# Decoder trunk on one core: second layer's tokens reordered in blocks of 128, softmax statistics exchanged by VectorE transposes, eleven query pairs projected ahead instead of eight

## The chip, the core and the metric

The kernel is one program on one core of a Trainium2 chip. Five engines run their own instruction queues in order and meet at semaphores: PE (TensorE, matrix products into PSUM), DVE (VectorE), ACT (ScalarE), POOL (GpSimd) and SP (SyncE, which here only issues DMA transfers). The metric is device time in microseconds of one execution; a smaller time is better. Before the change it is 1128.27 us, the median of three runs (1128.21, 1128.27, 1128.74).

## The reference

A sequence of 1024 tokens with 1024 features goes through two layers. The first is gated linear attention with 4 heads. The second is attention with 8 query heads over one shared set of keys and values (2 key/value heads), and it alone matters for most of the change:

```python
SWA_GROUPS = ((128, 1), (512, 4), (2048, 16))       # (window, dilation)
...
for gi, (window, dilation) in enumerate(SWA_GROUPS):
    o_g, lse_g = dilated_window_attention(q[:, :, gi], k_sh[:, :, gi], v_sh[:, :, gi], window, dilation)
    outs.append(o_g)
    lses.append(lse_g)
wts = jax.nn.softmax(jnp.stack(lses, axis=0), axis=0)
o = jnp.sum(wts[..., None] * jnp.stack(outs, axis=0), axis=0)
...
return (o.astype(x.dtype) * jax.nn.silu(g)) @ w_out
```

Each query head attends three times: with every token, with every 4th and with every 16th (groups 0, 1 and 2). Each gives an output, a row maximum and a row sum. A softmax over the three log-sums weighs the three outputs of a token. So the statistics of one token, which the three groups compute in three orders of the tokens, have to meet in one place, and the weights have to go back to each group's order.

## The kernel before, in words

Activations lie features by tokens, 128 features on the partitions. A projection is a product of three matmuls per block of 128 features (`mm3`): a float32 operand is split into a high and a low float32r half, and high x high, high x low and low x high are summed. `project` makes one head's projection, 2 halves of 512 tokens x 8 blocks x 3 = 48 matmuls of 128x512. `seven` makes the projections of two heads together with 7 products in place of 8 (sums of quarters of the weights and of the activations): 7 x 4 x 3 = 84 matmuls in place of 96. The list `EARLY` (line 42) names the query heads and groups that go through `seven` ahead of the attention; their results are written to DRAM (`qd`) and loaded again as `Q`. Before, it holds 8 pairs, groups 2 and 1 of all eight heads, so group 0 is left to `project`, one head at a time, inside the attention loop. With 3 pairs of keys there are 11 jobs.

The program's stages by the trace: first layer to about 436 us, the values and sums for `seven` to 503, the `seven` jobs to 712.4, attention to about 1029, and the output projection with the last normalization to the end.

Attention runs head by head (u = 0 to 7). `scores(u)` computes for each group and block the products of queries and keys (PSUM tiles `lv`, two of them), then on DVE adds the mask (`bmask`, `rmask`) and finds the row's extreme in one instruction, then on ACT takes the exponential and its row sum. Extremes and sums go to `sts` (groups 0 and 1) and `nat` (group 2). Then before the change SP moves them: `sts` to DRAM (`std`), from there to `nat` in the order of group 2; DVE and ACT make the weights `ew`; SP writes them to DRAM (`cwd`) and loads them as `cw` in the orders of groups 0 and 1. `attend(u)` multiplies each block `P` by its weight (16 instructions on whichever of DVE, ACT and POOL), transposes blocks on PE (`ms`), copies with triangle masks (`PT`), multiplies with the values into `po`, and adds into `og`. `g_proj(u)` projects the gate (48 matmuls, PSUM tile `acc`) and multiplies it in. `scores(u+1)` is recorded ahead of `attend(u)`.

The order on each engine is not written by hand. Every operation is recorded, and `Sched.order` (a planner with a table of costs, `cost`, and of latencies) places them one by one: at each step the operation that can start first, by program order where several can. Operations recorded under `vp`, `va` or `vap` may go to one of two or three engines, whichever the planner finds ends first. All instructions are issued from one line (465), so the trace is read by the names of the tiles.

Tiles of `small(..., "a", n)` are a pool of n buffers of 128x512: the `P` of groups 1 and 2, sums, and two diagonal blocks.

Of the kernel before, what the change touches and what calls it, by code (L numbers as in the profile page):

```python
# [53 lines left out]
def _rearr(x, pattern, **sizes):  # L54
# [567 lines left out]
def trunk(tc, xT, wP, wA, wA12, wAv3, w2, wO, wK, wV0, wV12, wB, wOB, par_d,  # L622
# [126 lines left out]
    def og_page(kt, pool):  # L749
# [5 lines left out]
        return ogs[kt]  # L755

    def layer_a(t2, t1, after):
# [46 lines left out]
        def evac_g(h, c, half, acc):  # L804
            S.vector.tensor_copy(H[h]["sg"][:, c, hs(half)], acc)
# [210 lines left out]
        def chunks(h, g):  # L1016
# [6 lines left out]
            for c in range(4):  # L1023
                cc = 4 * g + c
                cs = slice(c * 128, c * 128 + 128)
                for e in range(2):
                    es = slice(e * 128, e * 128 + 128)
                    S.tensor.matmul(po[e][:, cs], v[g][:, c, es], AT[:, cc, :], start=True, stop=(cc == 0))
                    if cc:
                        S.tensor.matmul(po[e][:, cs], St[:, es], blk(qe, cc), start=False, stop=True)  # L1030
# [70 lines left out]
    def out_ln(layer, r, w_of, res, emit):  # L1101
# [14 lines left out]
        for et in range(NK):  # L1116
# [4 lines left out]
            t = small("rt", "a", 13)[:, :n]  # L1121
# [29 lines left out]
    def out_ln_rows(j, wo, gam, bet):  # L1151
        xr = [small("res", tag, 2) for tag in ("t1", "t2")]
        rt = [small("rt", "a", 13) for _ in range(2)]
# [19 lines left out]
        mv = hp.tile([128, 2], F32, name="lnmv", bufs=2)  # L1173
        S.vector.bn_aggr(out=mv, in_=st)
        R = hp.tile([128, 1], F32, name="lnR", bufs=2)
# [16 lines left out]
    vd = dram.tile([T, 256], F32, name="vd")  # L1192
    vd3 = [dram.tile([T, 128], F32, name=f"vd3{c}") for c in range(2)]
    ogB = [dram.tile([128, T], F32, name=f"ogB{k}") for k in range(NK)]
    std = [dram.tile([2, 2, T], F32, name=f"std{k}") for k in range(NK)]
    cwd = [dram.tile([2, T], F32, name=f"cwd{k}") for k in range(NK)]
    DIL = (1, 4, 8)
# [3 lines left out]
    def to_group(pg, g, half):  # L1201
        if g == 2:
            return pg.rearrange("p (e a n) -> p n a e", e=16, a=8)[:, half * 4:half * 4 + 4]
        n = 512 // DIL[g]
        return pg.rearrange("p (r i) -> p i r", r=DIL[g])[:, half * n:half * n + n, :]

    def tok_view(ap, g):
        if g == 2:
            return ap.rearrange("p (n a e) -> p n a e", n=4, a=8)
        return ap.rearrange("p (i r) -> p i r", r=DIL[g])  # L1210

    def layer_b(xs, early):
        bmask = hp.tile([128, 256], F32, name="bmask", bufs=1)
# [4 lines left out]
        above, below = (p1.tile([128, 1, 128], U8, name=n, bufs=1) for n in ("above", "below"))  # L1218
# [632 lines left out]
```

## Time and profile before

| | |
|---|---|
| runs | 1128.21, 1128.27, 1128.74 us |
| profiled execution | 1128.91 us, span 1127.1 us, 20068 instructions |
| granted TensorE clock | 0.999 |
| busy: PE, PE weight load, DVE, ACT, POOL | 99%, 84%, 73%, 53%, 19% |
| DMA | 145.12 MB in 106768 packets, 45136 of them under 512 B |

The profiled execution is 1.81 us longer than its span and 0.64 us over the median of the runs. A matmul's record is longer than the distance to the next one's start, since matmuls overlap; what a matmul adds to the time is read from how many start in a stretch. "Busy" is the time in which at least one instruction of the engine runs. A wait row says which engine waited, at which tile, for which engine's work on which tile.

### The profile page before, as it was taken

To read this page: it belongs to the slowest core of one execution; us is meant where nothing else is said; L and a number is where in the kernel's file an instruction comes from. 1 tells how busy PE (TensorE), PEld (TensorE's weight loads), DVE (VectorE), ACT (ScalarE), POOL (GpSimd) and SP (SyncE) were. 2 spreads that over 40 slices of the span, in tenths; PEclk is the share of its full clock that TensorE was granted. 3 is DMA by queue.
4 is the path that set the end of the run, shared out by engine and by line. 5 is a ranking of instruction groups with operands and counts; after the bars stand their busy time and mean duration, and the time that the engine had idled before them with its cause. 6 is when DMAs were issued, how large, how long until landed. Compare 5 with 4: busy or idle time off the path is not lost.

```text
span 1127.1 us, 20068 instructions
## 1 busy us (share of the span) xinstructions
PE 1115.3 (99%) x7648; PEld 950.0 (84%) x7648; DVE 826.0 (73%) x1646; ACT 597.7 (53%) x1199; POOL 214.4 (19%) x209
## 2 busy tenths in 40 slices
PE   9999999999999999999999999999999999999997
PEld 9888888888988888998888888878888888888876
DVE  6286862687968489897888888567875767776578
ACT  5355542546464256666556656476664666643252
POOL 1000100112122031232223232322221123312010
PEclk9999999999999999999999999999999999999999
DMA  7211132221152444865656566955445553442644
GB/s 258 75 39 39 57 95 75 75 76 39 60 191 84 143 163 155 272 193 138 176 133 170 133 175 171 274 111 100 96 111 136 139 127 77 98 120 77 186 134 175
DMA packets 106768, 145.12 MB, mean 129 GB/s; under 512 B 45136, under 2 KB 63440, under 8 KB 106672
## 3 DMA queue, kind: packets, MB, share of 16 engines
q1 hardware_dynamic: 100192, 128.11, 36.5%
q0 software_dynamic: 6480, 15.73, 8.1%
q8 instruction: 60, 0.98, 0.4%
q14 instruction: 36, 0.29, 0.1%
HBM read 112.15 MB, written 31.65 MB: 128 GB/s over the span
## 4 chain that ended last, share of the span: by engine, by line
PE 91%; DVE 4%; DMA 2%; ACT 2%; issue 1%; POOL 0%; SPq 0%; DVEq 0%; ACTq 0%
PE acc L465 42%; PE sev L465 19%; PE po L465 9%; PE lv L465 8%; PE vac L465 7%; PE ms L465 4%; PE pro L465 2%; DMA wf<-in_wOB 1%; DVE P L465 1%; DVE rt L465 1%; DVE wl L465 1%; DVE t L465 0%; DMA xf<-in_xT 0%; DVE x1l L465 0%; ACT t L465 0%
## 5 line engine op out<-in xcount | busy, mean ns | idle before, releaser
L465 ACT ACTIVATE wh<-wf 128x1024 fp32r<-128x1024 f32 (+3 forms) x115 | 105.4, 919 | 159.9 <-PE acc L465 97.3
L465 PE MATMUL acc<-x1h,wh 128*128 128x512 f32 x256 | 114.0, 445 | 0.0
L465 PE MATMUL sev<-T,wh 128*128 128x512 f32 x352 | 108.3, 389 | 0.0
L465 DVE TENSOR_TENSOR wl<-wf,wh 128x1024 fp32r<-128x1024 f32 (+3 forms) x61 | 73.9, 1213 | 42.4 <-ACT wh L465 32.3
L465 PE MATMUL acc<-xh,wh 128*128 128x512 f32 x256 | 101.8, 398 | 0.0
L465 PE MATMUL acc<-x1h,wl 128*128 128x512 f32 x256 | 100.6, 393 | 0.0
L465 PE MATMUL acc<-x1l,wh 128*128 128x512 f32 x256 | 100.1, 391 | 0.0
L465 PE MATMUL acc<-xh,wl 128*128 128x512 f32 x256 | 99.8, 390 | 0.0
L465 PE MATMUL acc<-xl,wh 128*128 128x512 f32 x256 | 99.8, 390 | 0.0
L465 PEld LDWEIGHTS sev<-T,wh 128*128 128x128 f32 x352 | 66.1, 188 | 13.7
L465 ACT ACTIVATE P<-P,sts 128x256 f32<-128x256 f32 (+1 forms) x128 | 59.7, 468 | 30.5 <-DVE sts L465 28.4
L465 POOL DMA_DIRECT2D wl<-in_wB x39 | 34.6, 887 | 209.5 <-ACT wl L465 207.9
L465 PE MATMUL lv<-K,Q 128*64 128x64 f32 (+2 forms) x512 | 71.3, 288 | 1.8 <-DVE sts L465 1.8
L465 PE MATMUL sev<-T,wl 128*128 128x512 f32 x176 | 68.5, 389 | 0.0
L465 PEld LDWEIGHTS lv<-K,Q 128*128 128x128 f32 (+1 forms) x512 | 54.0, 163 | 14.9 <-DVE sts L465 4.4
L465 DVE CUSTOM_DVE_ANT_0 P<-lv,bmask 128x256 f32<-128x256 f32 (+1 forms) x128 | 46.4, 377 | 21.5 <-PE lv L465 21.0
L465 PE MATMUL acc<-ogh,wh 128*128 128x512 f32 x152 | 60.1, 396 | 0.1
L465 PE MATMUL acc<-ogl,wh 128*128 128x512 f32 x152 | 59.3, 390 | 0.0
L465 PE MATMUL acc<-ogh,wl 128*128 128x512 f32 x152 | 59.2, 390 | 0.0
L465 POOL TENSOR_TENSOR wl<-wf,wh 128x1024 fp32r<-128x1024 f32 x10 | 24.2, 2418 | 181.4 <-PE ms L465 91.5
L465 PEld LDWEIGHTS acc<-x1h,wl 128*128 128x128 f32 x256 | 48.0, 188 | 10.8
L465 PEld LDWEIGHTS acc<-xh,wl 128*128 128x128 f32 x256 | 48.1, 188 | 10.3
(304 smaller groups left out, 2997.3 us busy)
## 6 DMA issues: line engine op xcount, KB each, us to landing
wf<-in_wB SPq DMA_DIRECT2D x32, 512.0 KB
wf<-in_wA SPq DMA_DIRECT2D x24, 512.0 KB
wf<-in_wO SPq DMA_DIRECT2D x16, 512.0 KB
qd<-pair SPq DMA_DIRECT2D x16, 512.0 KB
Q<-qd SPq DMA_DIRECT2D x16, 512.0 KB
wf<-in_wOB SPq DMA_DIRECT2D x16, 512.0 KB
wl<-in_wB POOLq DMA_DIRECT2D x15, 512.0 KB, 7.8
wf<-in_wV SPq DMA_DIRECT2D x12, 512.0 KB
```

Of the source, the lines that this page charges most:

```text
L465: getattr(handle[o.eng], meth)(*[conv(a) for a in args], **{k: conv(v) for k, v in kw.items()})
```

## The change

Four things, made together.

1. **Order of tokens.** From the output of the first layer's heads on, the 128 tokens of each block stand in another order (16 x 2 x 4 read as 2 x 16 x 4). The first layer writes it: `evac_g` copies the gate out of PSUM in that order, and `chunks` lets PE write its outputs with runs of 4 elements. The residual input, the tables of the rotation, and the masks are given in that order from the host (`xp`, `cos`, `sin`, `bmask`, `tri`), and the host puts the rows back at the end.
2. **Statistics.** In the new order the tokens of one group that another group has on other partitions stay inside blocks of 32 partitions. A new function `swap` spreads the statistics over columns with a 0/1 mask (`swm`), transposes 32x32 blocks on DVE, and a `tensor_reduce` picks them up. Groups 1 and 2 are swapped to the order of group 0, and two swaps bring the weights back. All of the DMA transfers through `std` and `cwd` are gone. Group 0's weights are read from `ew` directly.
3. **Pairs ahead.** `EARLY` gets (2, 3, 0), (4, 5, 0) and (6, 7, 0): 14 jobs of `seven` in place of 11, and `project` for group 0 of heads 0 and 1 alone.
4. **Buffers.** The pool "a" has 12 buffers, not 13; `sts` and `nat` one each, not two; `cw` two, not one. Values of group 1 are stored and loaded in rows of the new order.

```diff
+NA = 12
-EARLY = [(0, 1, 2), (2, 3, 2), (0, 1, 1), (2, 3, 1), (4, 5, 2), (6, 7, 2), (4, 5, 1), (6, 7, 1)]
+EARLY = [(0, 1, 2), (2, 3, 2), (0, 1, 1), (2, 3, 1), (4, 5, 2), (6, 7, 2), (4, 5, 1), (6, 7, 1), (2, 3, 0), (4, 5, 0), (6, 7, 0)]
...
         def evac_g(h, c, half, acc):
-            S.vector.tensor_copy(H[h]["sg"][:, c, hs(half)], acc)
+            S.vector.tensor_copy(H[h]["sg"][:, c, hs(half)].rearrange("p (n s x r) -> p n s x r", n=4, s=2, x=16),
+                                 acc.rearrange("p (n x s r) -> p n s x r", n=4, x=16, s=2))
...
-                    S.tensor.matmul(po[e][:, cs], v[g][:, c, es], AT[:, cc, :], start=True, stop=(cc == 0))
+                    out = po[e][:, cs].rearrange("p (s x r) -> p x s r", s=2, x=16)
+                    S.tensor.matmul(out, v[g][:, c, es], natural(AT[:, cc, :]), start=True, stop=(cc == 0))
...
+        def swap(parts):
+
+            n = sum(w for _, w, _ in parts)
+            x, y = (hp.tile([128, 128], F32, name=i, bufs=1)[:, :n * 32] for i in ("swx", "swy"))
+            o = 0
+            for src, w, k in parts:
+                r = 32 // k
+                S.vp.tensor_mul(x[:, o:o + w * 32].rearrange("p (w k r) -> p w k r", w=w, k=k),
+                                src.rearrange("p (w r) -> p w r", w=w)[:, :, None, :].to_broadcast([128, w, k, r]),
+                                swm[k][:, None, :, None].to_broadcast([128, w, k, r]))
+                o += w * 32
+            S.vector.transpose(y, x)
...
-            dst = std[u]
-            with S.landing(RUNS):
-                for s in range(2):
-                    S.sync.dma_start(dst[1, s].rearrange("(n p r) -> p n r", n=2, r=4),
-                                      sts[:, s, 8:16].rearrange("p (n r) -> p n r", r=4))
...
+            flat = sts.rearrange("p g s c -> p (g s c)")
+            for (y,), i, w in ((swap([(flat[:, 16:32], 2, 4)]), 2, 2), (swap([(flat[:, 0:16], 4, 8)]), 1, 4)):
+                S.vector.tensor_reduce(out=nat[:, :, i].rearrange("p s (m c) -> p s m c", m=w // 2),
+                                       in_=y.rearrange("p (s m) r k -> p s m r k", s=2), op=OP.add, axis=AX.X)
...
-            with S.landing(GATHER):
-                S.sync.dma_start(cw[:, 0:8], cwd[u][0].rearrange("(n p) -> p n", p=128))
...
+            for y, c in zip(swap([(ew[:, 2], 1, 4), (ew[:, 1], 2, 8)]), (8, 0)):
+                w = y.shape[1]
+                S.vector.tensor_reduce(out=cw[:, c:c + 8].rearrange("p (w r) -> p w r", w=w), in_=y, op=OP.add, axis=AX.X)
...
-                    S.vap.scale(x, x, cw[:, column(g, j):column(g, j) + 1])
+                    c = column(g, j)
+                    S.vap.scale(x, x, cw[:, c:c + 1] if g else ew[:, 0, c:c + 1])
...
-                    ov = [po[i].rearrange("p (i r) -> p r i", r=4)[:, r, :] for i in range(2)]
+                    ov = [po[m].rearrange("p (n x r) -> p r x n", n=4, x=32)[:, r] for m in range(2)]
```

How the planner's order differs is shown at two places, with rows of the instruction order; "waits" names the semaphores a row waits for (DMAHW is a transfer, Pool, PE, DVE and Activation are engines).

VectorE, the exchange of one head's statistics before (head 2: the small operations on `cw`, `ew`, `nat` between score rows of the next head, `ISA P...<-lv`):

```order
L465 TENSOR_REDUCE cw_8187<-nat_7761 128x8 [waits DMAHW4_49,DMAHW7_49,DMAHW2_49,DMAHW0_49]
L465 ISA P_8189,sts_8133<-lv_8175,bmask_3562 128x128 [waits PE_49]
L465 ISA sts_8133 128x1
L465 TENSOR_TENSOR ew_8196<-cw_8187,nat_7761 128x24 [waits DVE_49]
L465 COPY_PREDICATED P_8132<-above_4912,P_8132 128x128 [waits Activation_49]
L465 TENSOR_TENSOR og_8103<-po_8126,og_8103 128x512 [waits PE_49]
L465 TENSOR_TENSOR nat_7761<-ew_8196,nat_7761 128x24 [waits DMAHW3_49,DMAHW5_49,DMAHW1_49,Activation_49]
```

VectorE now, the weights of head 1 (`ew`), the transpose that waits for POOL's `swx`, and the start of head 2's scores (`lv_8222`):

```order
L466 RECIPROCAL cw_8239<-cw_8239 128x8 [waits DVE_49]
L466 ISA P_8260,sts_8261<-lv_8222,rmask_3564 128x64
L466 ISA sts_8261 128x1
L466 TENSOR_TENSOR ew_8245<-ew_8245,cw_8239 128x24 [waits DVE_49]
L466 ISA P_8260,sts_8261<-lv_8222,rmask_3564 128x64
L466 ISA sts_8261 128x1
L466 TENSOR_TENSOR og_8158<-po_8173,og_8158 128x512 [waits DMAHW2_49,PE_49]
L466 STREAM_TRANSPOSE swy_8284<-swx_8273 128x96 [waits Pool_49]
L466 ISA P_8260,sts_8261<-lv_8222,rmask_3564 128x64
L466 ISA sts_8261 128x1
L466 TENSOR_REDUCE cw_8239<-swy_8284 128x8 [waits DVE_49]
L466 TENSOR_REDUCE cw_8239<-swy_8284 128x8
```

What waited for transfers now waits for DVE itself, ACT and POOL, and two transposes with their reductions have joined the same queue as the scores.

GpSimd before, the weights of head 2 multiplied into `P` and the masked copies `PT` that follow:

```order
L465 TENSOR_SCALAR P_7922<-P_7922,cw_8187 128x128 [waits DMAHW4_49,DMAHW3_49]
L465 TENSOR_SCALAR P_7922<-P_7922,cw_8187 128x256 [waits DVE_49]
L465 TENSOR_SCALAR P_7831<-P_7831,cw_8187 128x256 [waits DMAHW4_49,DVE_49]
L465 TENSOR_SCALAR P_7893<-P_7893,cw_8187 128x256
L465 TENSOR_SCALAR P_7898<-P_7898,cw_8187 128x256 [waits DMAHW2_49]
L465 TENSOR_TENSOR PT_8348<-P_7797,ident_316 128x128 [waits Activation_49]
```

GpSimd now, the same of head 1; `swx_8340` is the first swap of head 2's statistics:

```order
L466 TENSOR_TENSOR swx_8273<-ew_8245,par_321 128x32 [waits DVE_49,Pool_49]
L466 TENSOR_TENSOR swx_8273<-ew_8245,par_321 128x64
L466 TENSOR_SCALAR P_8111<-P_8111,ew_8245 128x256 [waits DMAHW4_49,Activation_49]
L466 TENSOR_SCALAR P_8111<-P_8111,ew_8245 128x256 [waits Activation_49]
L466 TENSOR_SCALAR P_8163<-P_8163,ew_8245 128x256 [waits Activation_49]
L466 TENSOR_SCALAR P_8009<-P_8009,cw_8239 128x128 [waits DVE_49]
L466 TENSOR_SCALAR P_8009<-P_8009,cw_8239 128x256
L466 TENSOR_SCALAR P_8026<-P_8026,cw_8239 128x256
L466 TENSOR_SCALAR P_8069<-P_8069,cw_8239 128x256
L466 TENSOR_SCALAR P_8080<-P_8080,cw_8239 128x128
L466 TENSOR_TENSOR swx_8340<-sts_8261,par_321 128x64 [waits Activation_49,Pool_49]
L466 TENSOR_TENSOR PT_8344<-P_8009,ident_316 128x128 [waits PE_49,Pool_49]
```

POOL has eight products with weights in place of five, with the masks of two swaps ahead of and behind them. Over the whole program POOL's products with weights go from 33 to 74, DVE's from 52 to 3, ACT's from 43 to 51; `PT` products go from 29 to 13 on DVE and from 35 to 51 on POOL. On PE, matmuls `acc<-x1h/x1l` of 128x512 go from 768 to 480 and `sev` from 924 to 1176; all others stay in number.

More of the change, by code (lines that the diff above doesn't have):

```diff
@@ L1152, in out_ln_rows @@
         xr = [small("res", tag, 2) for tag in ("t1", "t2")]
-        rt = [small("rt", "a", 13) for _ in range(2)]
+        rt = [small("rt", "a", NA) for _ in range(2)]
         st = hp.tile([128, 4, 6], F32, name="lnst", bufs=1)
@@ L1216, in layer_b @@
         S.sync.dma_start(rmask, rmask_d)
[L1218 to L1224 removed]
+        masks = p1.tile([128, 2, 2, 128], U8, name="masks", bufs=1)
+        above, below = ([masks[:, g, i:i + 1] for g in range(2)] for i in range(2))
+        uptos = p1.tile([128, 2, 128], F32, name="upto", bufs=1)
+        upto = [uptos[:, g:g + 1] for g in range(2)]
+        tri = small("tri", "d", 4).rearrange("p (g i b) -> p g i b", g=2, i=2)
+        S.sync.dma_start(tri, tri_d[:, 0:4].rearrange("p (g i) b -> p g i b", g=2))
+        S.sync.dma_start(uptos, tri_d[:, 4:6])
+        S.vector.tensor_copy(masks, tri)
         cosT, sinT = spare(F32, "cosT"), spare(F32, "sinT")
@@ L1267, in total @@
                 def total(op, x, y):
-                    t = small("sum", "a", 13)
+                    t = small("sum", "a", NA)
                     op(t, x, y)
@@ L1343, in proj_v0 @@
         def proj_v0(blocks):
-            pgs = [small("V0", "a", 13) for _ in range(2)]
+            pgs = [small("V0", "a", NA) for _ in range(2)]
             def evac(j, acc):
                 S.scalar.activation(blk(pgs[0], j % 4), acc[:, 0:128], AF.Copy)
-                S.vector.tensor_copy(blk(pgs[1], j % 4), acc[:, 128:256])
+                S.va.copy(blk(pgs[1], j % 4), acc[:, 128:256])
             project_tok(wV0, xs, [(j, lambda x, j=j: blk(x, j)) for j in blocks], evac)
@@ L1471, in scores @@
             P = {}
-            sts = hp.tile([128, 2, 16], F32, name="sts", bufs=2)
-            nat = hp.tile([128, 2, 3, 8], F32, name="nat", bufs=2)
+            sts = hp.tile([128, 2, 2, 8], F32, name="sts", bufs=1)
+            nat = hp.tile([128, 2, 3, 8], F32, name="nat", bufs=1)
             for g in (2, 1, 0):
@@ L1478, in scores @@
                     if g:
-                        p = small("P", "a", 13)
+                        p = small("P", "a", NA)
                     else:
@@ L1495, in scores @@
                         col = column(g, j)
-                        least, mass = (nat[:, i, 2, j:j + 1] if g == 2 else sts[:, i, col:col + 1] for i in range(2))
+                        least, mass = (sts[:, g - 1, i, col:col + 1] if g else nat[:, i, 0, j:j + 1] for i in range(2))
                         if g == 2:
@@ L1503, in scores @@
                                              start=True, stop=True)
-                        mk = rmask if g == 2 else bmask[:, 256 - nk:]
+                        mk = rmask if g == 2 else bmask[:, g, 256 - nk:]
                         S.vector.tensor_tensor_reduce(
@@ L1642, in attend @@
                 S.vector.tensor_add(og[:, hs(i)], po[i], og[:, hs(i)])
-        diag = [small("diag", "a", 13) for _ in range(2)]
+        diag = [small("diag", "a", NA) for _ in range(2)]
         for x in diag:
@@ L1652, in layer_b @@
             if u == 3:
-                with S.behind(cwd[3]):
-                    reload_k(1)
+                reload_k(1)
             scores(u + 1)
@@ L1673, in reload_og @@
             for kt in range(6):
-                load_og(ogA[kt], kt, p0, lambda: small("ogf", "a", 13), (half,))
+                load_og(ogA[kt], kt, p0, lambda: small("ogf", "a", NA), (half,))
     layer_a(t2, t1, reload_og)
@@ L1729, in early @@
                 with S.later(-EVAC):
-                    load_og(ogB[kt], kt, p0, lambda: small("ogf", "a", 13), (half,))
+                    load_og(ogB[kt], kt, p0, lambda: small("ogf", "a", NA), (half,))
     U = layer_b(x1s, early)
@@ L1734, in trunk @@
         for kt in range(4, 6):
-            load_og(ogB[kt], kt, p1, lambda: small("ogf", "a", 13), (half,))
+            load_og(ogB[kt], kt, p1, lambda: small("ogf", "a", NA), (half,))
         for u in (6, 7):
@@ L1763, in trunk, with _positions @@
     return S
+def _positions():
+    import numpy as np
+    return np.arange(1024).reshape(8, 16, 2, 4).transpose(0, 2, 1, 3).ravel()
 def _arrays(inputs):
```

146 lines of the change are left out of this document (69 added, 77 removed).

## The prediction

> **What bounds the kernel now.** I read the page first, then the stages by windows, then PE's waits, then groups by form. The page says one engine never rests, and the chain of waits runs through it:
>
> ```profile
> PE 1115.3 (99%) x7648; PEld 950.0 (84%) x7648; DVE 826.0 (73%) x1646; ACT 597.7 (53%) x1199; POOL 214.4 (19%) x209
> PE 91%; DVE 4%; DMA 2%; ACT 2%; issue 1%; POOL 0%; SPq 0%; DVEq 0%; ACTq 0%
> ```
>
> A share over the whole span could hide stages, so I cut it: the `seven` jobs, the attention, the end, and five pieces of the attention. The columns are the piece, its length, then busy us of PE, PEld, DVE, ACT and POOL with instruction counts, the granted clock, the DMA share and GB/s:
>
> ```profile
> 503.00:712.40 209.40, 209.40 (x927) 173.40 (x926) 170.05 (x247) 126.57 (x218) 58.32 (x57) 1.00 0.61 162
> 713.00:1029.00 316.00, 314.21 (x1994) 271.70 (x1994) 226.73 (x767) 186.99 (x576) 78.06 (x103) 1.00 0.49 118
> 1029.00:1127.00 98.00, 89.98 (x418) 74.88 (x416) 67.30 (x101) 33.00 (x46) 3.68 (x2) 0.98 0.48 159
> 767.00:811.00 44.00, 43.80 (x307) 37.70 (x306) 34.90 (x133) 29.77 (x97) 13.66 (x22) 1.00 0.49 111
> 811.00:857.00 46.00, 46.00 (x289) 41.13 (x289) 32.85 (x102) 22.91 (x71) 7.54 (x12) 1.00 0.38 82
> 857.00:905.00 48.00, 47.40 (x318) 40.96 (x317) 33.30 (x130) 28.46 (x100) 7.42 (x8) 1.00 0.55 150
> 905.00:950.00 45.00, 45.00 (x278) 38.89 (x278) 32.41 (x117) 28.01 (x81) 10.96 (x15) 1.00 0.41 81
> 950.00:985.00 35.00, 34.85 (x246) 30.96 (x245) 26.95 (x100) 25.14 (x87) 15.55 (x24) 1.00 0.55 126
> ```
>
> PE fills every stage but the end at full clock. DVE is second: 72% of the attention (226.73 of 316.00), 79% in its densest piece (34.90 of 44.00), and even there PE loses only 0.20 us. PE's and the weight loads' whole waits in the attention are these, and none of them names a transfer, while DVE waits for PE far longer:
>
> ```profile
> PE lv L465 <- DVE sts L465: 1.8, 5, 0.6
> PEld lv L465 <- DVE sts L465: 4.4, 6, 1.0
> DVE P L465 <- PE lv L465: 25.0, 33, 2.0
> POOL P L465 <- DMA cw<-cwd: 29.1, 5, 12.8
> ```
>
> So the statistics' trip through DRAM stops POOL (29.1 us) but not PE. Time here is the sum of PE's work plus a few us in which DVE frees `lv` too late.
>
> **The change part by part.** *Pairs ahead.* PE loses 288 matmuls of `project` (6 heads x 48) and gains 252 of `seven` (3 jobs x 84). A matmul's price is how many start in a stretch that holds only such: the `seven` stage above gives 209.40 / 927 = 0.226 us; a stretch of pure projection gives 17.00 / 75 = 0.227 us:
>
> ```profile
> 712.60:729.60 17.00, 17.00 (x75) 13.89 (x74) 1.86 (x3) 2.37 (x4) 1.00 0.91 267
> ```
>
> That is -288 x 0.227 = -65.3 and +252 x 0.226 = +56.9, together **-8.4 us**. The `seven` stage grows by 56.9 us and the attention shrinks to 316 - 65.3 = 250.7 us. In the `seven` stage DVE is at 170.05 of 209.40 (81%) over 11 jobs and PE lost nothing, so three more of the same kind, whose last sums lie contiguous, are taken as free; without that cover a job could lose a few tenths of a us, about 1 us in all.
>
> *Order of tokens on PE.* Matmuls of the first layer now write runs of 4 floats, 16 B, apart. Of the `po<-PT` matmuls before, those of group 1 already write single floats 16 B apart, and the row shows no spread worth a term:
>
> ```profile
> L465 PE MATMUL po<-PT,V x432: 270/275/377, 780.6 to 1027.3; 128*128 128x128 f32 x144
> ```
>
> I take 0. `evac_g` reads PSUM in short runs, 16 instructions; DVE's plain copy and its strided sum bound it:
>
> ```profile
> L465 DVE COPY sg<-acc 128x512 f32<-128x512 f32 x16 | 11.0, 688 | 28.9 <-PE acc L465 28.9
> L465 DVE TENSOR_TENSOR pair<-t,t 128x512 f32<-128x512 f32 x34 | 36.9, 1091 | 5.5 <-DMA qd<-pair 3.2 <-POOL t L465 2.0
> ```
>
> At most 16 x 0.4 = 6.4 us more on DVE, in a place where that group waits 28.9 us for PE: 0 on the path.
>
> *The exchange.* 160 transfers leave SP; PE waited for none, so their going is worth 0, and what is late next is DVE's own chain. That chain joins the queue of the scores, so I sum DVE's load in the attention. It loses and gains by these rows:
>
> ```profile
> L465 DVE TENSOR_SCALAR P<-P,cw 128x256 f32<-128x256 f32 x37 | 13.5, 408 | 0.1
> L465 DVE TENSOR_SCALAR P<-P,cw 128x128 f32<-128x128 f32 x15 | 4.2, 295 | 1.2 <-DMA cw<-cwd 1.2
> L465 DVE TENSOR_TENSOR t<-acc,cosT 128x512 f32<-128x512 f32 x16 | 11.1, 691 | 11.4 <-PE acc L465 7.7 <-ACT t L465 3.7
> L465 DVE TENSOR_TENSOR Q<-t,t 128x512 f32<-128x512 f32 x8 | 5.8, 720 | 0.1
> L465 DVE TENSOR_TENSOR t<-t,sinT 128x512 f32<-128x512 f32 x14 | 12.3, 876 | 9.1 <-ACT t L465 9.0
> L465 DVE TENSOR_TENSOR PT<-P,ident 128x256 f32<-128x256 f32 x15 | 6.2, 442 | 0.0
> L465 DVE TENSOR_TENSOR PT<-P,ident 128x128 f32<-128x128 f32 x14 | 5.3, 387 | 5.1 <-PE po L465 5.1
> L465 DVE TENSOR_REDUCE cw<-nat 128x8 f32<-128x24 f32 x16 | 2.8, 174 | 0.1
> L465 DVE DVE_READ_ACCUMULATOR2_ANT sts<- 128x1 f32 x128 | 10.5, 82 | 0.0
> L465 DVE COPY_PREDICATED P<-above,P 128x128 f32<-128x128 uint8 x40 | 16.0, 409 | 4.6 <-ACT P L465 4.2
> ```
>
> It loses 34 x 0.408 + 15 x 0.295 (weights), 12 x 0.691 + 6 x 0.720 + 8 x 0.876 (rotation of six heads), 8 x 0.442 + 8 x 0.387 (`PT`) = 44.5 us. It gains 24 transposes, 32 reductions and 8 products, all small. No row shows such a transpose: between 0.082 (an accumulator read) and 0.409 us (a 128x128 copy under a mask) I take 0.2, next to the 0.174 of the small reduction: 64 x 0.2 = 12.8 us, bounds 5.2 and 26.2. DVE comes to 226.7 - 44.5 + 12.8 = 195 us of 250.7, 78%, at worst 208 (83%). The piece at 79% shows PE unhurt at that density. [...]
>
> *What moves to POOL.* Its products with weights go from 33 to 74. Rows of the attention and of the whole program:
>
> ```profile
> L465 POOL TENSOR_SCALAR P<-P,cw 128x256 f32<-128x256 f32 x23 | 15.6, 824 | 0.2 <-DMA cw<-cwd 0.2
> L465 POOL TENSOR_SCALAR P<-P,cw 128x128 f32<-128x128 f32 x10 | 5.9, 618 | 29.0 <-DMA cw<-cwd 29.0
> L465 POOL TENSOR_SCALAR P<-P,cw x33: 367/617/1902, 771.7 to 979.3; 128x256 f32<-128x256 f32 x23, 128x128 f32<-128x128 f32 x10
> L465 DVE CUSTOM_DVE_ANT_0 P<-lv,bmask 128x256 f32<-128x256 f32 x88 | 35.9, 419 | 18.3 <-PE lv L465 17.9
> L465 DVE CUSTOM_DVE_ANT_0 P<-lv,bmask 128x128 f32<-128x128 f32 x40 | 11.3, 285 | 3.2 <-PE lv L465 3.1
> L465 DVE CUSTOM_DVE_ANT_0 P<-lv,rmask 128x64 f32<-128x64 f32 x64 | 10.9, 219 | 4.0 <-PE lv L465 4.0
> L465 DVE TENSOR_TENSOR og<-po,og 128x512 f32<-128x512 f32 x16 | 11.0, 687 | 4.6 <-PE po L465 4.3
> L465 DVE SCALAR_TENSOR_TENSOR og<-og,sg 128x512 f32<-128x512 f32 x15 | 12.7, 845 | 0.1
> ```
>
> On average POOL has room, but one place is tight: the DVE transpose that waits for `swx_8340`. On POOL that swap stands behind two other swap products, six weights of 256 and two of 128: with 0.37 (the shortest row) for a swap product, 3 x 0.37 + 6 x 0.824 + 2 x 0.618 = 7.3 us after `ew` is done. In the same stretch DVE has six scores of 64 columns, two of 128 and one of 256, each with an accumulator read of 0.082 (6 x 0.301 + 2 x 0.367 + 0.501 = 3.0), two sums into `og` (1.4), three products with the gate (3 x 0.845 = 2.5) and three small operations of the exchange (0.6): 7.5 us. Near a draw: DVE, and with it the scores queued behind (`P_8354` and the `lv` bank that PE waits for), loses between 0 and 1.5 us per head; I take 0.5 over six or seven heads, **+3 us**. [...]
>
> *Buffers.* One `P` buffer less and single `sts` and `nat` tiles tie neighbouring heads closer. Two heads' `P` of groups 1 and 2 need ten with the two diagonals, and there are 12; 0, or inside the bound of the wait above.
>
> **Sum.** 1128.9 (the profiled execution) - 8.4 + 3 = 1123.5; it stands 0.6 over the median, so 1122.9, rounded to **1123 us** for a median of runs.
>
> **The rivals.**
>
> *A. PE alone decides.* The waits of 1.8 and 4.4 us do not grow, since DVE's and POOL's waits for transfers are gone and fall where DVE has slack. Then 1128.3 - 8.4 = 1119.9, 1120 us, and down to 1117 if half of the old waits go too. For it: DVE waits 25 us for `lv`, so it has slack. Against it: less filler between scores.
>
> *B. GpSimd gates the scores (slower).* The place is the transpose behind `swx_8340`; if the six to eight weights ahead of it take 1.2 us each instead of 0.8, DVE stands 3 us per head, 7 heads 21 us, and the time is 1128 - 8 + 21 = 1141. From 8.4 / 7 = 1.2 us of lost time per head on, the kernel is no faster. For it: the 1902 ns record, and PE's fillers in the attention cut from 768 to 480. Against: DVE's own load there sinks by 30 us, so POOL meets it less often. [...]
>
> *C. The gain is lost ahead of the attention.* The strided copies of the first layer or the three new jobs hold PE up by 6 to 9 us: 1127 to 1130. Only the 81% of DVE in the `seven` stage speaks for it; PE's 209.40 of 209.40 speaks against.
>
> That the transfers stay or the matmuls do not fall is no rival: the counts of the new order show both gone.
>
> **How the numbers follow.** Forecast (1120.5 to 1127) 0.55; A 0.20; B 0.20; C 0.05. About 0.2%, 2.3 us, is what measurement tells from no change. Faster (under 1126): all of A and most of the forecast's range, 0.20 + 0.47 = 0.67. Same: the forecast's upper end 0.08, C, and the light end of B, 0.16 together. Slower: the rest of B, 0.17. The range leaves out half of B's upper end and a little below A: 1117.5 to 1132. The forecast's own range is 1120.5 to 1127.
>
> **What would show it.** In the new profile: 1176 `sev` matmuls in about 266 us with PE full; attention in 251 us plus the waits; PE's and PEld's waits for `DVE sts` at 5 to 10 us; DVE near 78% there; the transposes near 0.2 us. Waits of DVE for POOL `swx` over 1.2 us per head would say B. A PE that is idle in the `seven` stage would say C. The forecast is wrong if the matmul work does not fall by 8 us or if any wait in the attention grows past 8 us.

## The result and the profile after

The changed kernel takes **1121.2 us** (median of four runs, 1121.03 to 1121.77), the kernel before 1128.24 beside it (1128.04 to 1128.74). The ratio is 0.9938, 95% interval 0.9921 to 0.9955: 7.0 us less. The profiled execution took 1121.77 us with a span of 1120.0 us, 7.1 us shorter than the span before.

The page of the changed kernel, PE's part of the first line and the packets: 36 matmuls fewer, and small packets almost gone.

```profile
PE 1107.7 (99%) x7612; PEld 943.8 (84%) x7612; DVE 842.7 (75%) x1670; ACT 609.4 (54%) x1237; POOL 267.0 (24%) x300
DMA packets 69921, 150.57 MB, mean 134 GB/s; under 512 B 6880, under 2 KB 23904, under 8 KB 69824
```

The three stages that the change touches, by windows of the changed kernel (piece, length, then busy us and instructions of PE, PEld, DVE, ACT, POOL, the granted clock, the DMA share and GB/s):

```profile
503.80:773.28 269.48, 268.38 (x1177) 220.38 (x1176) 218.30 (x301) 162.02 (x279) 103.77 (x88) 1.00 0.59 158
773.50:1023.50 250.00, 248.65 (x1712) 219.19 (x1711) 201.82 (x743) 162.50 (x547) 92.69 (x166) 1.00 0.44 135
1023.50:1112.50 89.00, 88.87 (x414) 74.16 (x412) 63.14 (x94) 32.73 (x45) 5.04 (x3) 1.00 0.51 165
```

From the starts of the first and last matmuls of each stage, the span's -7.1 us splits into +0.7 up to the `seven` stage, +60.2 in it (209.25 to 269.48), -67.4 in the attention (317.35 to 250.0), and -0.8 from there to the last matmul; 0.1 lies behind that. The attention is now 250 us long, PE is busy in 248.65 of them, and DVE stands at 201.82, 81%.

The waits of the changed kernel (engine and tile, for whose work on which tile: us in total, times, longest). The three long ones of GpSimd are a queue that is early, not one that is waited for; VectorE waits for its products 1.1 us in the whole program, never more than 0.3:

```profile
POOL swx L466 <- DVE ew L466: 22.7, 4, 8.8
POOL swx L466 <- DVE sts L466: 20.9, 3, 9.0
POOL swx L466 <- ACT P L466: 20.9, 7, 5.3
PEld lv L466 <- DVE sts L466: 2.8, 4, 1.7
PE lv L466 <- DVE sts L466: 1.2, 1, 1.2
DVE swy L466 <- POOL swx L466: 1.1, 5, 0.3
PE sev L466 <- ACT u L466: 0.6, 1, 0.6
PE sev L466 <- DVE wl L466: 0.5, 1, 0.5
```

PE's and its weight loads' waits for `sts` are 1.2 and 2.8 us, where they were 1.8 and 4.4. The instructions of the exchange, by tile (ns: shortest, median, longest; then first and last start):

```profile
L466 DVE STREAM_TRANSPOSE swy<-swx x24: 233/278/314, 796.0 to 1006.3; 128x64 f32<-128x64 f32 x8, 128x128 f32<-128x128 f32 x8, 128x96 f32<-128x96 f32 x8
L466 POOL TENSOR_TENSOR swx<-ew,par x14: 230/264/297, 814.4 to 974.2; 128x32 f32<-128x32 f32 x7, 128x64 f32<-128x64 f32 x7
L466 POOL TENSOR_TENSOR swx<-sts,par x10: 288/404/542, 803.2 to 987.0; 128x128 f32<-128x128 f32 x6, 128x64 f32<-128x64 f32 x4
```

And GpSimd's products of `P` with the weights, 74 in place of 33, which became shorter (median 478 ns, 617 before):

```profile
L466 POOL TENSOR_SCALAR P<-P,cw x40: 362/478/1516, 816.1 to 1007.5; 128x256 f32<-128x256 f32 x22, 128x128 f32<-128x128 f32 x18
L466 POOL TENSOR_SCALAR P<-P,ew x34: 368/478/1087, 814.9 to 1006.0; 128x256 f32<-128x256 f32 x32, 128x128 f32<-128x128 f32 x2
```

One head's exchange on VectorE, from the timeline of the changed kernel (start, us, instruction): 6.7 us from the first sum of group 2's statistics to the last of the weights. What took a trip through DRAM twice is now a row of instructions of 0.2 to 0.4 us.

```profile
861.73 0.25 DVE L466 TENSOR_REDUCE nat<-swy 128x16 f32<-128x64 f32 x1
862.01 0.31 DVE L466 STREAM_TRANSPOSE swy<-swx 128x128 f32<-128x128 f32 x1
862.83 0.37 DVE L466 TENSOR_REDUCE nat<-swy 128x16 f32<-128x128 f32 x1
863.73 0.17 DVE L466 TENSOR_REDUCE cw<-nat 128x8 f32<-128x24 f32 x1
...
865.95 0.18 DVE L466 TENSOR_TENSOR ew<-ew,cw 128x24 f32<-128x24 f32 x1
867.78 0.27 DVE L466 STREAM_TRANSPOSE swy<-swx 128x96 f32<-128x96 f32 x1
868.09 0.38 DVE L466 TENSOR_REDUCE cw<-swy 128x8 f32<-128x32 f32 x2
```

### The profile page after: what moved, and what is told of

Same layout as the page of the kernel before. It is cut to its first block, busy times and chain, and to the rows that moved or that the text cites. A ratio compares the mean times of both kernels' runs of the same rounds, so it can differ in the third digit from the quotient of the medians.

```text
span 1120.0 us, 20000 instructions
## 1 busy us (share of the span) xinstructions
PE 1107.7 (99%) x7612; PEld 943.8 (84%) x7612; DVE 842.7 (75%) x1670; ACT 609.4 (54%) x1237; POOL 267.0 (24%) x300
## 5 line engine op out<-in xcount | busy, mean ns | idle before, releaser
L466 PE MATMUL sev<-T,wh 128*128 128x512 f32 x448 | 138.1, 390 | 0.0
L466 PEld LDWEIGHTS sev<-T,wh 128*128 128x128 f32 x448 | 84.1, 188 | 17.6 <-ACT wh L466 0.3
L466 PE MATMUL sev<-T,wl 128*128 128x512 f32 x224 | 87.5, 390 | 0.5 <-DVE wl L466 0.5
L466 PE MATMUL acc<-x1h,wh 128*128 128x512 f32 x160 | 71.1, 444 | 0.0
L466 PE MATMUL acc<-x1h,wl 128*128 128x512 f32 x160 | 62.9, 393 | 0.0
L466 PE MATMUL acc<-x1l,wh 128*128 128x512 f32 x160 | 62.6, 391 | 0.0
L466 ACT ACTIVATE P<-P,sts 128x64 f32<-128x64 f32 (+2 forms) x128 | 50.1, 393 | 22.8 <-DVE sts L466 21.5
L466 POOL TENSOR_TENSOR wl<-wf,wh 128x1024 fp32r<-128x1024 f32 x9 | 21.5, 2389 | 159.9 <-PE ms L466 91.5
L466 POOL DMA_DIRECT2D wl<-in_wB x42 | 37.0, 896 | 86.3 <-ACT wl L466 84.5
L466 PEld LDWEIGHTS acc<-xh,wl 128*128 128x128 f32 x256 | 48.1, 188 | 10.2
L466 PEld LDWEIGHTS po<-PT,V 128*128 128x128 f32 x432 | 54.3, 192 | 2.6 <-ACT og L466 0.2
```

The source lines that it names most:

```text
L466: getattr(handle[o.eng], meth)(*[conv(a) for a in args], **{k: conv(v) for k, v in kw.items()})
```

## The experiments

My theory: PE's matmul work sets the time; the pairs ahead bring 8.4 us of it, and the exchange, which PE never waited for, is worth nothing by itself. The rivals: the exchange itself pays or costs; it is only the exchange that lets the pairs pay; GpSimd is on the path of the scores. In all of them the planner places the instructions anew, except where the text says that the order is the same.

### The two halves of the change, one at a time

The changed kernel with the old list of pairs:

```diff
-EARLY = [..., (4, 5, 1), (6, 7, 1), (2, 3, 0), (4, 5, 0), (6, 7, 0)]
+EARLY = [..., (4, 5, 1), (6, 7, 1)]
```

> The changed kernel with the old list of eight pairs: the new order of tokens and the exchange on VectorE, without the pairs ahead. First theory (PE's matmul work sets the time, the exchange is worth nothing either way): 1128.2 us as before, at most 1 us more for the slower matmuls on the weights s, so 1127.5 to 1129.5, ratio to before 0.9995 to 1.001, and PE's waits for VectorE's sts in the attention at most 6 us. Rival (the exchange itself pays: PE's waits of 6.2 us go with the transfers): 1122 to 1125. Second rival (the exchange costs PE a few us and only the pairs hide it): 1131 or more.

Measured: 1129.0 us, ratio to before 1.0005 (0.9996 to 1.0014). So order of tokens, exchange and buffers together are worth nothing in time: by the starts of the stages the `seven` stage takes 2.8 us more (212.08 us against 209.25), the attention 2.2 us less (315.1 against 317.35), the end 0.8 less.

The kernel before with the three pairs added, and nothing else:

```diff
-EARLY = [..., (4, 5, 1), (6, 7, 1)]
+EARLY = [..., (4, 5, 1), (6, 7, 1), (2, 3, 0), (4, 5, 0), (6, 7, 0)]
```

> The kernel before with the three pairs of group 0 added and nothing else: statistics still go through DRAM, the token order is the old one. First theory (the trip through DRAM never reached PE, so the pairs are worth the same without the exchange): 1128.2 - 8.4 + 0 to 1.5 = 1120 to 1121.5, within 1 us of the changed kernel. Rival (288 matmuls fewer between the scores leave the trip of 12 us uncovered, the products with cw come late and PE stands 1 to 3 us per head): 1125 to 1140, with PE waits on PT, po or lv that name GpSimd, VectorE or a transfer.

Measured: **1153.9 us**, ratio 1.0225 (1.0208 to 1.0243). Not 8 us faster, but 25.7 slower: my theory falls here, and the rival's mechanism is seen, beyond its upper time. GpSimd's waits for the weights, 29.1 us before, are now

```profile
POOL P L465 <- DMA cw<-cwd: 73.3, 6, 19.7
PE ms L465 <- ACT P L465: 6.4, 4, 2.3
PE ms L465 <- DVE P L465: 5.8, 2, 4.6
```

and PE stands at `ms`, the transposes of `P`, which must be weighted first. One half alone gives +0.8 us, the other +25.7, both together -7.0: the exchange (with the order of tokens and the buffers, which came with it) brings nothing until the projections leave the attention, and then it is worth 1153.9 - 1121.2 = 32.7 us.

The two runs also take the `seven` stage apart. Its window with the old order of tokens and 14 jobs, then with the new order and 11:

```profile
504.37:770.73 266.36, 266.36 (x1178) 220.54 (x1177) 215.88 (x317) 160.94 (x277) 72.60 (x70) 1.00 0.60 160
503.72:715.80 212.08, 210.95 (x926) 172.94 (x925) 171.09 (x235) 127.25 (x219) 82.75 (x70) 1.00 0.60 160
```

In the old order three more jobs cost 266.36 - 209.25 = 57.1 us, and PE never pauses. The changed kernel needs 3.1 us more for the same jobs (269.48). 2.8 us of that are there with 11 jobs already, so they come with the new order, exchange or buffers, not with the jobs.

Whether a single pair would still have been free, with the kernel before and (6, 7, 0) alone:

```diff
+EARLY = [..., (4, 5, 1), (6, 7, 1), (6, 7, 0)]
```

> The kernel before with one pair added, (6, 7, 0), and the statistics still through DRAM: 96 matmuls of project go, 84 of seven come, -2.7 us. Theory (each projection taken out of the attention costs more than it brings as long as a head's statistics take some 25 us to travel; three pairs lost 32 us, so one loses about a third): 1128.3 - 2.7 + 5 to 12 = 1131 to 1138 us. Rival (there is a threshold: the first pair is free, only the later ones, which take the work of the first heads, stop PE): 1125 to 1127 us.

Measured: 1135.2 us, ratio 1.0066 (1.0054 to 1.0079). This one pair already costs 7 us where its matmuls save 2.7. So with the trip through DRAM this pair is not free; no other single pair was tried.

### Is it the time of the trip?

The changed kernel, whose statistics and weights also go to DRAM and come back unchanged. No engine but SP gets work:

```diff
+        def trip(x, name):
+            n = x.shape[1] // 8
+            d = dram.tile([n, 128, 8], F32, name=name)
+            with S.landing(RUNS):
+                for i in range(n):
+                    S.sync.dma_start(d[i], x[:, i * 8:i * 8 + 8])
+                for i in range(n):
+                    S.sync.dma_start(x[:, i * 8:i * 8 + 8], d[i])
...
             flat = sts.rearrange("p g s c -> p (g s c)")
+            trip(flat, f"std{u}")
...
+            trip(cw, f"cwd{u}")
```

> The changed kernel with eleven pairs and its exchange on VectorE, in which the statistics sts and the weights cw also go to DRAM and back unchanged, per head 4 and 2 transfers out and as many back on SP's queue, with nothing else on any engine; the planner knows of them. First theory (with eleven pairs it is the time of the trip that stops PE; that is why the kernel before with eleven pairs takes 1153.9): 5 us or more from the product to the weights, PE waits of 10 to 35 us in the attention, 1135 to 1156 us. Rival (the trip is hidden, the kernel before with eleven pairs is slow for its order of tokens, its buffers or its SP queue): 1121 to 1126 us.

Measured: 1127.25 us, 6 us over the changed kernel, below the 1135 to 1156 us of the first theory and just over the rival's 1126: unclear alone. The trace shows why it is small. Only the weights are delayed much (6.9 us a head against 1.8, the statistics 3.7 against 1.9, in the table below); the statistics of groups 1 and 2 set out while group 0 is still being scored, and group 0's do not travel at all in the new order.

```profile
POOL P L466 <- DMA cw<-cwd: 19.8, 4, 7.0
PE lv L466 <- DVE sts L466: 2.6, 3, 1.4
```

So a larger dose: the whole of `nat`, group 0 too, and `cw`, each twice there and back (`times=2` in `trip`, called on `nat` behind the swaps and on `cw`).

> As trip2, with a larger dose: per head the whole of nat (all three groups, after the swaps) goes to DRAM and back twice in a row, and so do the weights cw. In the kernel before with eleven pairs the statistics came 7 to 18 us behind the last exponential and the weights 5 to 13 us behind the product; in trip2 only 2 to 6 and 6 to 8 us. First theory (with eleven pairs PE stands once the whole trip of a head is some 20 us; the order of tokens and the buffers have no part in it): about 10 us for the statistics and 12 for the weights, and 1140 to 1156 us, near the 1153.9 of the kernel before with eleven pairs. Rival (trip2's 6 us are nearly all that latency costs, the rest of the 32 us is the old order of tokens, the old buffers or another order of instructions): 1127 to 1133 us.

Measured: 1193.9 us, ratio 1.0576 (1.0563 to 1.0590): above both ranges, since the dose came out larger than I meant. VectorE and ScalarE wait for the weights, and PE for `P`, and once for a load of `Q`:

```profile
ACT P L466 <- DMA cw<-cwd: 40.9, 5, 17.8
DVE P L466 <- DMA cw<-cwd: 37.6, 4, 16.2
PE ms L466 <- DVE P L466: 33.2, 4, 10.1
PE lv L466 <- DMA Q<-qd: 9.7, 1, 9.7
```

The doses can be compared by two waits worked out from the records, as means over the eight heads: from the end of a head's last exponential to VectorE's first small reduction (`cw<-nat`), and from the product that makes `ew` to the first `P` that is multiplied with `cw`.

| kernel | pairs | statistics, us | weights, us | sum | time |
|---|---|---|---|---|---|
| before | 8 | 13.1 | 8.1 | 21.2 | 1128.2 |
| changed, 8 pairs | 8 | 1.9 | 2.4 | 4.3 | 1129.0 |
| before, 9 pairs | 9 | 13.2 | 8.9 | 22.1 | 1135.2 |
| changed | 11 | 1.9 | 1.8 | 3.7 | 1121.2 |
| changed, one trip | 11 | 3.7 | 6.9 | 10.6 | 1127.3 |
| before, 11 pairs | 11 | 12.6 | 7.5 | 20.1 | 1153.9 |
| changed, two trips | 11 | 18.2 | 14.0 | 32.2 | 1193.9 |

With eight pairs, 21.2 against 4.3 us of delay per head change nothing. With eleven, 7 us more per head cost 6 us of time, 16 us cost 33, and 28 us cost 73: slowly at first, then about 3 us of time for each us of delay per head. Not all of the 73 is delay. 9.7 us are one wait for `Q`, whose load goes through the same SP queue as the added transfers, and 68 us of that run's profiled execution passed at a granted clock of one half (the mean of the whole is 0.97; see the last section). By an estimate, half of that time, these alone can cost up to 34. The kernel before with eleven pairs lies near the line between its neighbours (35 us by it, 33 measured), so its old order of tokens and its buffers need no part in it; no run tries them apart, and a line through two points that far from each other is a weak measure.

### GpSimd on the path

The same order of instructions; GpSimd executes the first product of each weights' exchange 13 times:

```diff
+                    again = o.eng == "POOL" and o.writes[0].buf.name == "swx" and o.reads[0].buf.name == "ew" and o.writes[0].shape[1] == 1
+                    for _ in range(13 if again else 1):
-                    getattr(handle[o.eng], meth)(...)
+                        getattr(handle[o.eng], meth)(...)
```

> The changed kernel in which GpSimd executes the first product of each weights' exchange (swx<-ew, 0.264 us) 13 times instead of once, with the same result: 12 x 0.264 = 3.2 us more ahead of VectorE's transpose, in seven heads, 22 us in all on GpSimd. The order of all other instructions is the same. Theory (VectorE reaches that transpose late or PE has slack behind it): VectorE waits for swx 1 to 2.5 us per head, but of that PE loses less than half: 1121 to 1128 us. Rival B of the prediction (GpSimd gates the scores, each us of wait is lost): 7 x 2.7 = 19 us, 1138 to 1142 us.

Measured: **1143.75 us**, ratio 1.0136 (1.0122 to 1.0149), just above the rival's range. GpSimd's products for the weights of head 0 in this kernel and in the changed one (start, us, instruction), then the waits of this kernel:

```profile
814.11 4.32 POOL L468 TENSOR_TENSOR swx<-ew,par 128x32 f32<-128x32 f32 x14 [8.29 <-DVE sts L468]
814.40 0.49 POOL L466 TENSOR_TENSOR swx<-ew,par 128x32 f32<-128x32 f32 x2 [8.29 <-DVE sts L466]
```

```profile
DVE swy L468 <- POOL swx L468: 27.5, 9, 4.1
PE lv L468 <- DVE sts L468: 17.2, 9, 2.6
```

The 12 added products take 3.8 us per head, 0.32 each from start to start. VectorE's transpose starts 2.9 to 3.8 us later behind the product that makes `ew`, 25.6 us in the seven heads together, and the attention grew by 20.8 (from 250.0 to 270.8). Rival B's mechanism is real and has little slack: at this dose, each us that GpSimd is late costs 0.8 us of PE. In the changed kernel its price is near zero because GpSimd is there in time. By the measure of the table above the weights come only 4.9 us behind the product here, against 6.9 with one trip, which cost 6 us. There the planner had ordered the instructions with the trip in view; here the order is the old one, and VectorE stands at the transpose, with the scores of the next head behind it. So the delay alone doesn't set the price; what queues behind it does too.

The opposite, all products of the exchange on VectorE:

```diff
-                S.vp.tensor_mul(x[:, o:o + w * 32]...
+                S.vector.tensor_mul(x[:, o:o + w * 32]...
```

> The changed kernel with all products of the exchange on VectorE, none on GpSimd: 24 products of 0.19 to 0.4 us more on VectorE, about 7 us in 250, and VectorE's transposes wait for nothing but VectorE. First theory (the hop over GpSimd costs VectorE 1.1 us of waits and PE nothing): 1120 to 1123 us. Rival B (the hop is on the path, as 3.2 us more on it cost 22 us): 2 to 4 us faster, 1117 to 1119.5. Third (VectorE is near its limit): slower than 1124.

Measured: 1125.76 us, ratio to before 0.9975 (0.9965 to 0.9985), 4.6 us over the changed kernel. The time lies in the third theory's range, but its reason isn't shown: the planner moved other work off VectorE, which is busy for 843.8 us in all, against 842.7 in the changed kernel. The trace shows one long stall in its place. The first row is PE's wait; the second a masked copy of VectorE by its tiles (ns: shortest, median, longest); then two rows of GpSimd's timeline, and the window behind the stall:

```profile
PE lv L466 <- DVE sts L466: 2.7, 2, 2.3
L466 DVE COPY_PREDICATED P<-masks,P x64: 286/308/3791, 797.3 to 1003.9; 128x128 f32<-128x128 uint8 x40, 128x256 f32<-128x256 uint8 x24
848.20 2.21 POOL L466 TENSOR_SCALAR P<-P,cw 128x256 f32<-128x256 f32 x5
850.15 1.89 POOL L466 TENSOR_TENSOR PT<-P,ident 128x128 f32<-128x128 f32 x4
853.94:857.35 3.41, 3.41 (x10) 2.67 (x9) 2.55 (x11) 2.30 (x8) 0.00 (x0) 0.50 0.93 310
```

The copy that took 3791 ns ran from 848.42 to 852.21, while GpSimd executed nine instructions without a pause, to 852.04. A score stood behind it, PE waited 2.3 us for that, and from 853.94 on the granted clock was 0.50 for 3.4 us. The profiled execution's span is 4.2 us longer: 2.0 us more of it is idle PE, and 3.4 us at half clock cost, by an estimate, at most half of that, 1.7. So by this trace most of the price is this one VectorE copy of 3.79 us beside GpSimd's work, where the median is 0.31, and what followed it, not a fuller VectorE; no run takes that copy out. The changed kernel has a shorter one, a copy of 2.39 us at 821, ahead of PE's wait of 1.2 us for `sts`.

### How far the pairs go

The changed kernel with the twelfth pair:

```diff
+EARLY = [..., (4, 5, 1), (6, 7, 1), (0, 1, 0), (2, 3, 0), (4, 5, 0), (6, 7, 0)]
```

> The changed kernel with the twelfth pair (0, 1, 0) added: 96 matmuls of project go, 84 of seven come, -12 x 0.227 = -2.7 us. First theory (PE's work decides here too): 1121.2 - 2.7 = 1118.5, 1117.5 to 1119.5. Rival (the 17 us of pure projection at the start of the attention cover the loading of Q, K and V and the first scores; without them PE waits 3 to 10 us there): 1121.5 to 1129, with PE idle just behind the last seven matmul.

Measured: 1138.4 us, ratio 1.0083 (1.0070 to 1.0097): 17 us slower than with eleven, not 2.7 faster. PE's first long wait behind the `seven` stage is the rival's, 2.7 us for a load of `Q`, but it is a small part of the 17. Two reasons are possible, number or place. The same number as the changed kernel, at another place:

```diff
-EARLY = [..., (4, 5, 1), (6, 7, 1), (2, 3, 0), (4, 5, 0), (6, 7, 0)]
+EARLY = [..., (4, 5, 1), (6, 7, 1), (0, 1, 0), (2, 3, 0), (4, 5, 0)]
```

> The changed kernel with another eleventh pair: (0, 1, 0) in place of (6, 7, 0), so heads 6 and 7 are projected inside the attention, not heads 0 and 1. The number of matmuls is that of the changed kernel. First theory (the twelfth pair cost 17 us because the work between the scores ran out in number; eleven pairs leave enough wherever it lies): 1120 to 1124 us. Rival (the place decides: without the projections of heads 0 and 1 the first heads have nothing between their scores, and PE stands there): 2 to 3 us over the kernel with twelve pairs or near it, 1132 to 1141 us, with PE's waits before 890 us of the span.

Measured: 1139.3 us, ratio 1.0094 (1.0078 to 1.0109). The number is the same and the time is 18 us longer: the place decides. The first 100 us from about the first score on, in three kernels (changed, this one, twelve pairs): PE is idle for 1.25 us in the first, 7.7 in the others, and gets through 691 matmuls against 598 and 608.

```profile
790.50:890.50 100.00, 98.75 (x691) 86.89 (x691) 79.47 (x327) 70.72 (x250) 36.37 (x68) 1.00 0.44 134
```

```profile
778.00:878.00 100.00, 92.34 (x598) 76.77 (x598) 72.34 (x316) 64.11 (x234) 23.80 (x47) 0.95 0.47 148
```

```profile
798.00:898.00 100.00, 92.28 (x608) 77.04 (x609) 72.87 (x318) 65.01 (x237) 23.78 (x47) 0.97 0.49 154
```

These 100 us hold most of the loss, not all. In the whole execution PE of the second kernel is idle for 10.5 us more than in the changed one, 6.4 of them here; 2.3 us are one wait at 961, behind another VectorE copy that took 3.8 us while GpSimd worked.

So I tried twelve pairs with other work for the first heads, the gate's projections two heads early:

```diff
+        def g_early(u):
+            def evac(half, acc):
+                sg = small("sg", "t2", 2)
+                sigmoid_gate(sg, acc)
+                S.sync.dma_start(gd[u][:, hs(half)], sg)
+            project(wB[u, 3], xs, evac, added=True)
...
+        g_early(0)
         scores(0)
         q_proj(1)
+        g_early(1)
...
-            if 0 < u < 5:
-                g_proj(u - 1)
+            if u:
+                g_late(u - 1)
+            if 0 < u < 5:
+                g_early(u + 1)
```

> The changed kernel with twelve pairs and the gate's projections of heads 0 to 5 moved ahead by two heads: those of heads 0 and 1 stand where the projections of the queries of heads 0 and 1 stood, their results go to DRAM and are loaded when og is there. First theory (twelve pairs lost only because the first heads had nothing between their scores): 1121.2 - 2.7 = 1118.5, up to 1121 with a stall or two. Rival (eight projections are too few for the eight heads wherever they lie, since VectorE's 187 us and the exchange fill the 228 us that PE would take): 1124 to 1138 us, with PE's waits moved to heads 5 to 7.

Measured: 1137.3 us (1132.0 to 1139.3), ratio 1.0067 (1.0049 to 1.0085). The time is in the rival's range: it does not pay. The profiled execution is the fastest of the six (1132.0 us), so the trace shows less than the median lost. In its first 100 us PE is idle for 5.2, and the rest of its stalls are at 985 us and in the last head:

```profile
803.00:903.00 100.00, 94.82 (x650) 80.11 (x649) 73.25 (x322) 68.45 (x248) 27.52 (x54) 1.00 0.53 163
```

Eight projections are too few here with this order; whether a better order of the same eight would do is open. No kernel of mine beats the changed one by more than a measurement tells.

### The weights that start later

In the `seven` stage, matmuls with the weights `s` start 233 ns apart on average (228 to 236), most others and nearly all of before 226 or 227 (the records of `sev<-x1h,s`: 389 ns before, 396 now). Two kernels with the order of the changed one, with the tiles moved: `s` by 64 bytes, and everything on the other side of the memory by 32.

```diff
-        mv = hp.tile([128, 4], F32, name="lnmv", bufs=2)
+        mv = hp.tile([128, 16], F32, name="lnmv", tag="cw", bufs=2)
```

> The changed kernel with the same instructions in the same order; the four buffers that hold the weights s (s4) move by 64 bytes, from 215232 to 215296, so that they begin at a multiple of 128 as in the kernel before. First theory (the place of s is why its 168 matmuls start 232 to 235 ns apart instead of 227): pitch back at 227 ns, the seven stage 1 to 1.4 us shorter, 1120.0 us, ratio to the changed kernel 0.999. Rival (the place doesn't matter; the pitch comes from what runs beside it): pitch stays 232 to 235, 1121.2 us.

```diff
-    epsc = const.tile([128, 1], F32, name="epsc")
+    epsc, onec = (lambda x: (x[:, 0:1], x[:, 1:2]))(const.tile([128, 2], F32, name="consts"))
...
-    onec = const.tile([128, 1], F32, name="onec")
```

> The changed kernel with epsc and onec in one tile, so that everything behind them on the left side of the memory (weights wh and wl, activations x1h and x1l, the T pages) begins 32 bytes earlier, at a multiple of 128 as in the kernel before; the weights s stay where they are (a multiple of 64). The order of instructions is the same. Theory (the 32 bytes that the larger par added on the left are why matmuls on s and x1 start 232 to 236 ns apart): all pitches in the seven stage back at 227 ns, that stage 1.2 to 1.8 us shorter, about 1119.5 us. Rival (not the place of the tiles, but for instance the strided order or what runs beside): pitch stays at 232 to 236 and the time at 1120.4 to 1121.2 us.

Measured: 1120.4 us (ratio to before 0.9932, 0.9919 to 0.9944) and 1121.5 (0.9941, 0.9929 to 0.9953), both the changed kernel's time. The rows of before, the changed kernel, and the two:

```profile
L465 PE MATMUL sev<-x1h,s 128*128 128x512 f32 x88 | 28.9, 389 | 0.0
```

```profile
L466 PE MATMUL sev<-x1h,s 128*128 128x512 f32 x112 | 37.5, 396 | 0.0
```

```profile
L466 PE MATMUL sev<-x1h,s 128*128 128x512 f32 x112 | 37.6, 397 | 0.0
```

```profile
L466 PE MATMUL sev<-x1h,s 128*128 128x512 f32 x112 | 37.5, 395 | 0.0
```

Both fail: it is not these 64 or 32 bytes. By the records of the changed kernel it is also not ScalarE or GpSimd: these starts are 233 ns apart on average with either of them busy beside the matmul, and without. VectorE works beside every one of them, so it isn't ruled out. 168 matmuls by 6 to 7 ns are 1.0 to 1.2 us; the cause stays open.

## Why the prediction was right, and where it was right for the wrong reason

The forecast of 1123 us and its range hold the 1121.2, and the sign is right. Step by step:

- **PE bounds the kernel.** Right: 248.65 busy of 250.0 us in the attention, 268.38 of 269.48 in the `seven` stage.
- **Pairs ahead, -8.4 us.** The matmuls did what was counted: the `seven` stage grew by 60.2, of which 57.1 are the three jobs (as in the kernel before with eleven pairs), against 56.9 forecast; the attention shrank by 67.4, 65.3 plus 2. But the step was written as a term of its own, and that is wrong: alone it is +25.7 us. The sentence "PE waited for none, so their going is worth 0" was read from a trace in which 768 fillers covered the trip. With 480, the lack of the exchange costs 33 us. The sum came out since both edits were in it: that the omission did no harm was luck.
- **The `seven` stage, 0 to 1 us lost.** Mis-sized: 3.1, and not for the reason given: the three jobs lose nothing in the old order, and 2.8 of the 3.1 are there without them in the new. Two stalls, at 515 and 647 us, where PE waits for the weights' rest `wl` and for `u`, each 0.7 us over the usual distance of starts, and 1.0 to 1.2 us of the slower weights `s`; the rest is not assigned. PE is idle for 1.1 us of the stage, the sign named for rival C; its size is a third to half of that rival's.
- **VectorE's load, 195 of 250.7 us.** 201.8 of 250.0, inside the bound of 208. The small operations were longer than the 0.2 taken: 0.278 a transpose, 0.17 to 0.38 a reduction. Whether a fuller VectorE would cost time isn't shown: the run meant for it left the load the same.
- **Waits of VectorE for `swx`, 0.5 us a head, +3 us.** This step failed. They are 1.1 us in all, and PE's waits for `sts` fell. GpSimd's products with weights took 0.56 to 0.64 us on average for 256 columns and 0.54 for 128, where I had added 0.824 and 0.618, so it stood waiting ahead of its swap products.
- **Rival B.** Did not come, but its mechanism stands, and its point of turning lies near: 25.6 us of delay cost 20.8, so some 1.5 us per head would have eaten the 8.4, where 1.2 was forecast. The spread of GpSimd's products remains, 362 to 1516 ns, but the median fell from 617 to 478; that VectorE's fewer products of its own are the reason is only argued. Nor is it shown that VectorE's work beside them makes them long: the record of 1902 ns in the kernel before ran with VectorE busy from start to end, and so did the shortest one, of 367. For VectorE's own masked copies of `P` (128x128) the traces show a spread beside GpSimd: in the changed kernel the 27 with GpSimd idle took 291 to 308 ns, the six with GpSimd busy for over 90% of their time 306 to 2392; in the kernel before, 27 took 254 to 312 and ten 295 to 2995. With the exchange on VectorE one took 3791. Why some beside GpSimd are long and others not isn't shown.
- **Rival A.** Nearest, 1120 against 1121.2: PE's waits did not grow, and about 2 us of the old ones went; the `seven` stage took 3.1 back. The sign of being wrong, "any wait in the attention" past 8 us, is met to the letter by GpSimd's waits of over 20 us, but those are a queue that is early.
- **Order of tokens, buffers, 0.** Agrees in sum: with eight pairs the time is 0.8 us over the kernel before. In parts it does not: the `seven` stage is 2.8 us longer, the attention 2.2 shorter.

## What to carry to other kernels

That an engine waits for nothing holds only for the work that stands between: before you take filler out of a stage, add up the trips and chains that it covered, as the next wait is theirs. A change of two halves needs both runs, each half alone; here they give +0.8 and +25.7 us, and -7.0 together. And to learn whether a queue that is "near a draw" has slack, add a known delay to it: the slope, 0.8 us of time for each us of delay, tells more than the wait, which reads 1.1 us. And when work is moved between engines by a planner, compare the busy times before giving the load as the cause: VectorE's had not changed.

## What the hardware showed that I had not expected

In one kernel the time lost is more than the length of PE's stalls. The kernel before with eleven pairs executes the same 7612 matmuls as the changed one, yet its span is 34.4 us longer, of which only 17.0 are more idle time; the other 17.4 are more busy time for the same matmuls:

```profile
PE 1125.1 (97%) x7612; PEld 953.2 (83%) x7612; DVE 847.3 (73%) x1695; ACT 604.2 (52%) x1215; POOL 216.5 (19%) x210
```

The granted clock explains, by an estimate, up to 13.7 of these: it was half in four stretches of 3.4, 3.4, 10.2 and 10.2 us, 27.3 us together, and half of that is 13.7. The rest is not assigned. The stretch at half clock with the exchange on VectorE was 3.4 us long too. Below are windows of the kernel before with eleven pairs (the granted clock is the third column from the end) around its longest stall, 4.65 us at 959:

```profile
955.00:962.00 7.00, 4.37 (x14) 2.08 (x14) 5.44 (x28) 5.67 (x23) 0.00 (x0) 1.00 0.56 159
962.00:966.00 4.00, 1.09 (x4) 0.72 (x4) 1.88 (x7) 0.30 (x1) 0.00 (x0) 0.53 0.71 255
966.00:970.00 4.00, 3.02 (x14) 3.02 (x15) 0.43 (x1) 1.11 (x4) 0.00 (x0) 0.50 0.18 3
...
982.00:986.00 4.00, 4.00 (x21) 4.00 (x21) 1.34 (x9) 0.88 (x4) 0.80 (x2) 0.50 0.02 4
```

In the kernel with the other eleventh pair half clock followed a lighter gap, 4 us in which PE was busy for 2.40 by its records, which last longer than the distance between starts (389 to 397 ns against 226 to 236 in the `seven` stage):

```profile
844.00:848.00 4.00, 2.40 (x14) 1.56 (x11) 3.60 (x11) 4.00 (x22) 3.75 (x8) 0.99 0.77 235
848.00:851.00 3.00, 2.63 (x6) 1.70 (x7) 2.05 (x12) 2.33 (x11) 0.41 (x1) 0.50 1.00 239
```

So half clock began beside a wait of 4.65 us, behind a window in which PE's records are busy for 2.40 of 4 us, and, with the exchange on VectorE, behind a wait of 2.3 us. What it takes to bring it about is not shown; in the changed kernel, whose wait of 1.2 us was PE's longest for a score, the clock stayed at 1.00 through the attention. By the author's estimate, with half of the work done at a granted clock of 0.50, each stretch of 3.4 us costs up to 1.7 us on top of the stall. With eleven pairs and the trip through DRAM that is up to 13.7 of the 34.4 us.
